# One weight pool throughout, a down product that begins in freed tiles of h, x loaded once, gate and up interleaved k by k, and lo parts on GpSimd

## The chip, the cores and the metric

The kernel runs on one core of a Trainium2 chip. The metric is device microseconds of one execution. Before the change the median of three runs is 3011.32 us (3008.94 to 3018.25). The execution that was profiled took 3016.26 us, and its trace spans 3014.5 us.

## The reference

One decoder layer for 1024 tokens of width 1024, everything in float32. What matters here are the two SwiGLU layers (d_ff 2816, 22 blocks of 128 columns) at its two ends; between them lie three mixers that the change touches only through the weight pool.

```python
def _swiglu(h, w_gate, w_up, w_down):
    return (jax.nn.silu(h @ w_gate) * (h @ w_up)) @ w_down
...
    x = x + 0.5 * _swiglu(_rmsnorm(x, ffn1_norm[l]), ffn1_w_gate[l], ffn1_w_up[l], ffn1_w_down[l])
    h = _rmsnorm(x, mix_norm[l])
    p_rwkv, q_nsa, kv_nsa, g_nsa, q_mem, g_branch = _split(h @ w_in[l], IN_SPLITS)
    ...
    merged = (gb[:, :, 0] * (y_rwkv @ w_br_rwkv[l]) + gb[:, :, 1] * (y_nsa @ w_br_nsa[l]) + gb[:, :, 2] * (y_mem @ w_br_mem[l]))
    x = x + merged @ w_out[l]
    x = x + 0.5 * _swiglu(_rmsnorm(x, ffn2_norm[l]), ffn2_w_gate[l], ffn2_w_up[l], ffn2_w_down[l])
return _rmsnorm(x, final_norm)
```

## The kernel before

**Precision.** Every operand of a matmul is a pair: `split` (L74) writes the rounded value `hi` on ScalarE (L77) and the rest `lo = src - hi` on VectorE (L80). A product is three matmuls (`mm3`, L95: hi by hi L97, hi by lo L98, lo by hi L99). All tokens of a tile lie along the free axis, 512 ("a half") at a time, so nearly every instruction is on 128x512.

**Weights.** `wload` fetches a raw 128x512 piece over SP's queue (L84, tile `wraw`) and splits it into `whi`, `wlo`. The pool is opened anew by `open_w` (L60) for each of three stretches: 8 raw buffers and 4 pairs in the first SwiGLU, 2 and 3 in the mixers, 8 and 4 in the second SwiGLU. What is opened anew lies in memory that tiles of the stretch before used until then.

**A SwiGLU layer.** `Gates.plain` (L290) does the blocks f = 0 and 1 for one half of the tokens, gate and then up, eight k each. `Gates.sums` (L304) then makes, from h of both halves, four sums and differences of 128x512 tiles for each of four k (three on GpSimd, L311, L312, L314; one on VectorE, L313) and splits them into the tiles t1 to t4. `Gates.run` (L347) takes the other 20 blocks as seven products P1 to P7 in place of eight; P1, P2 and P3 read h, P5, P6, P7 and P4 read t1, t2, t3, t4. The block's weights need such sums too (`blocks`, L324, GpSimd, tiles `wS`). Results go as `sg` to DRAM (`ad<-sg`, L288). PSUM tiles are called `pgu`.

**Down.** `tail` (L185) reads `ad` back and splits it into tiles `a`, in four chunks (L21: 5 blocks in tiles of their own, 8 in the tiles of h, 5, and 4 in the tiles of h again). Per chunk and per d (eight blocks of 128 output columns) it multiplies with the down weights into PSUM tiles `pd` (four banks) and adds them to x in SBUF (L221). All eight tiles of x are loaded (L1496, L1702; 512 KB each) ahead of the first chunk.

**Start.** x's first half is loaded into ring tiles `rg`, normed without its rstd (`hu`), and used by `plain(0)`. x's second half is loaded when ring tiles come free, its squares are added up on GpSimd (L110), `rstd` (L113) has TensorE sum them over partitions (`nps`), and `plain(1)` follows. For the sums the first half is loaded a second time.

**Before the second SwiGLU.** The last rows of the merge (`h<-gbt`, L1589) are followed by the product with w_out (`wo`, weights from `in_wo`), into the ring again.

**Order.** A scheduler orders the instructions of each engine's queue from the program's tiles and pools; each engine then works its queue strictly in order. SP's queue issues nearly all DMAs.

Of the kernel before, what the change touches and what calls it, by code (L numbers as in the profile page):

```python
# [8 lines left out]
FT = mybir.dt.float32  # L9
# [8 lines left out]
D = 1024  # L18
KT = 8
HALF = 512  # L20
CHUNKS = (("p", 5), ("h", 8), ("p", 5), ("t", 4))  # L21
RING = 10
AHEAD = 3

# [4 lines left out]
class Builder:  # L29
    def __init__(self, ctx, tc, A):  # L30
        self.ctx, self.tc, self.nc, self.A = ctx, tc, tc.nc, A
        self.cst = ctx.enter_context(tc.tile_pool(name="cst", bufs=1))
        self.hp = ctx.enter_context(tc.tile_pool(name="hp", bufs=1))
        self.bg = []
        self.consts()
# [21 lines left out]
        self.eps = self.cst.tile([128, 1], FT, name="eps")  # L57
        nc.vector.memset(self.eps, 1e-6)

    def open_w(self, st, raw=2, parts=3):  # L60

        self.wp = st.enter_context(self.tc.tile_pool(name="wp", bufs=1, reuse_waits="tile"))
        self.wbufs = raw, parts

    def load_consts(self):
        nc, A = self.nc, self.A
# [13 lines left out]
        (nc.vector if eng_lo == "dve" else nc.gpsimd).tensor_sub(lo, src, hi.bitcast(FT))  # L80

    def wraw(self, src, n):
        raw = self.wp.tile([128, n], FT, name="wraw", tag="wraw", bufs=self.wbufs[0])
        self.nc.sync.dma_start(raw, src)  # L84
        return raw

    def wparts(self, raw, eng_lo="dve", eng_hi="act"):
        hi, lo = [self.wp.tile([128, raw.shape[-1]], FR, name=t, tag=t, bufs=self.wbufs[1]) for t in ("whi", "wlo")]
        self.split(hi, lo, raw, eng_hi, eng_lo)
        return hi, lo  # L90

# [93 lines left out]
    def tail(self, x, wd, ad, xload, after, aside=None, st=None):  # L185

        nc = self.nc
        halves = [slice(0, HALF), slice(HALF, S)]
        ap = st.enter_context(self.tc.tile_pool(name="ffa", bufs=1, reuse_waits="tile"))
        ps = st.enter_context(self.tc.tile_pool(name="ffd", bufs=1, space=PSUM, reuse_waits="tile"))  # L190

        def parts(kind, j):

            if kind == "p":
                return [[ap.tile([128, HALF], FR, name=f"a{p}{j}{half}") for p in range(2)] for half in range(2)]
            a, b = (1, j) if kind == "t" else divmod(j, 4)
            return [[self.hp.tile([128, HALF], FR, name=f"a{p}{j}{half}", tag=f"h{p}{a}{2 * b + half}")
                     for p in range(2)] for half in range(2)]

        def loads(kind, f0, n):  # L200
            got = []
            for j in range(n):
                t = parts(kind, j)
                for half in range(2):
                    raw = self.wraw(ad[f0 + j][half], HALF)
                    self.split(*t[half], raw)
                got.append(t)
                yield got

        def down(d, f0, a, hs):  # L210
            w = []
            for q0 in range(0, len(a), 4):
                q1 = min(q0 + 4, len(a))
                w.append(self.wload(wd[d, :, (f0 + q0) * 128:(f0 + q1) * 128], (q1 - q0) * 128))
            for half in hs:
                p = ps.tile([128, HALF], FT, name="pd", tag="dn", bufs=4)
                for j, t in enumerate(a):
                    wc = slice((j % 4) * 128, (j % 4) * 128 + 128)
                    self.mm3(p, [b[:, wc] for b in w[j // 4]], t[half], j == 0, j == len(a) - 1)
                c = halves[half]  # L220
                nc.vector.scalar_tensor_tensor(x[d][:, c], p, 0.25, x[d][:, c], op0=OP.mult, op1=OP.add)  # L221

        f0 = 0
        gens, at = [], []
        for kind, n in CHUNKS:
            gens.append(loads(kind, f0, n))
            at.append(f0)
            f0 += n
        a = [None] * len(CHUNKS)
        for a[0] in gens[0]:  # L230
            pass
        for d in range(KT):
            xload(d)
        for ci, (kind, n) in enumerate(CHUNKS):
            if ci < len(CHUNKS) - 1:
                for d in range(KT):
                    down(d, at[ci], a[ci], (0, 1))
                    a[ci + 1] = next(gens[ci + 1], a[ci + 1])
                    if aside and ci:
                        next(aside, None)  # L240
                if aside and ci:
                    for _ in aside:
                        pass
            else:
                for half in range(2):
                    for d in range(KT):
                        down(d, at[ci], a[ci], (half,))
                        self.tick()
                        after(half, d)


class Gates:
# [37 lines left out]
    def plain(self, half, h, r=lambda: None, loads=None, step=None):  # L290

        B = self.B
        for f in range(2):
            for gu in range(2):
                w = [loads.pop(0) if loads else B.wload(self.wgu[f, gu, q], 512) for q in range(2)]
                ps = self.bank()
                for k in range(KT):
                    wc = slice((k % 4) * 128, (k % 4) * 128 + 128)
                    B.mm3(ps, [a[:, wc] for a in w[k // 4]], h[k], k == 0, k == KT - 1)
                if step:  # L300
                    step()
                self.finish(f, half, gu, ps, r())

    def sums(self, h, k, raw):  # L304


        B, nc = self.B, self.nc
        a11, a12, a21, a22 = raw
        add = nc.gpsimd
        out = []  # L310
        add.tensor_sub(a11, a12, a11)  # L311
        add.tensor_sub(a12, a22, a12)  # L312
        nc.vector.tensor_sub(a22, a22, a11)  # L313
        add.tensor_sub(a21, a21, a22)  # L314
        for n, a in ((1, a11), (2, a22), (3, a12)):
            t = [self.tp.tile([128, HALF], FR, name=f"t{p}{n}{k}") for p in range(2)]
            B.split(*t, a)
            out.append(t)
        t = [B.hp.tile([128, HALF], FR, name=f"t{p}4{k}", tag=f"h{p}1{k}") for p in range(2)]
        B.split(*t, a21)  # L320
        out.append(t)
        return out

    def blocks(self, m):  # L324
# [1067 lines left out]
def body(ctx, tc, A, VO):  # L1392
# [44 lines left out]

    with ExitStack() as fs:
        with ExitStack() as st:
            B.open_w(fs, 8, 4)  # L1440
            ring = ring_of(st)
            F = Gates(B, st, ring, A["wgu1"], ad)
            g1 = VO["ffn1_norm"]
            hu, h = ([], []), ([], [])

            def loadx(half, k):
                t = ring()
                nc.sync.dma_start(t, A["xT"][k][:, halves[half]])
                return t

            xt, early, acc = [], [], None
            for k in range(KT):
                xt.append(loadx(0, k))
                if k in LOADS:
                    early.append(B.wload(A["wgu1"][0, LOADS[k][0], LOADS[k][1]], 512))
            for k in range(KT):
                t = F.temp()
                nc.vector.tensor_scalar(t, xt[k], B.vec[:, g1 + k:g1 + k + 1], None, op0=OP.mult)
                B.split(*B.htile(hu, 0, k), t)
                acc = B.add_square(np_, acc, xt[k], nc.gpsimd)  # L1460
            r = {}

            def more():
                if not r:
                    r[0] = B.rstd(np_, nps, acc)

            F.plain(0, hu[0], lambda: r[0], early, more)
            B.load_consts()
            xt, acc = [], None
            for k in range(KT):  # L1470
                xt.append(loadx(1, k))
                acc = B.add_square(np_, acc, xt[k], nc.gpsimd)
            r[1] = B.rstd(np_, nps, acc)
            for k in range(KT):
                B.normed(xt[k], xt[k], r[1], g1 + k)
                B.split(*B.htile(h, 1, k), xt[k])
            F.plain(1, h[1])
            sums, late = [], []
            for k in range(4):
                two = []  # L1480
                for j in (k, k + 4):
                    t = loadx(0, j)
                    B.normed(t, t, r[0], g1 + j)
                    hj = [B.hp.tile([128, HALF], FR, name=f"h{p}0{j}", tag=f"h{p}0{j}") for p in range(2)]
                    B.split(*hj, t)
                    two.append((hj, t))
                h[0].insert(k, two[0][0])
                h[0].append(two[1][0])
                sums.append(F.sums(h, k, (two[0][1], xt[k], two[1][1], xt[k + 4])))
            F.run(h, sums)  # L1490
        mt = met.enter_context(tc.tile_pool(name="met", bufs=1, side="right", reuse_waits="tile"))
        xp = xs.enter_context(tc.tile_pool(name="xp", bufs=1, side="right", reuse_waits="tile"))
# [6 lines left out]
                   M.tokens(mt, np_, nps, VO["mem_norm"]), st)  # L1499

    with ExitStack() as mid:
        B.open_w(mid)
        B.mmp = mid.enter_context(tc.tile_pool(name="mmp", bufs=1, space=PSUM, reuse_waits="tile"))
        gp = mid.enter_context(tc.tile_pool(name="gp", bufs=1, reuse_waits="tile"))
        sp = Spill(B, drp, A)
# [119 lines left out]

    with ExitStack() as fs:
        np_, nps = B.norm_pool(fs)
        B.open_w(fs, 8, 4)
        with ExitStack() as st:
            ring = ring_of(st)  # L1630
            xt, r, h = {}, {}, ([], [])
# [153 lines left out]
```

## Time and profile before

| | us |
|---|---|
| median of three runs | 3011.32 (3008.94 to 3018.25) |
| the profiled execution | 3016.26 |
| its span in the trace | 3014.5 |
| TensorE busy | 2842.3 (94 %) |
| VectorE, ScalarE, GpSimd busy | 1772.1, 1289.0, 640.7 (59, 43, 21 %) |

TensorE is busy 94 % of the span, in stretches that are wholly full and a few that are not. In the page's 40 slices the thin ones are the first two, the seventh, the 29th, the 37th and the last: the start, the two changes from gates to down, w_out and the sums, and the end. In a full stretch a matmul of 128x512 takes 0.2267 us (24 of them, one product of 4 blocks for two halves, 5.44 us).

### The profile page before, as it was taken

The page shows a single profiled execution, that of the slowest core. Times are in us where ns is not written, and L with a number is a line of the kernel's source. Part 1 is how long each engine was busy: PE and PEld are TensorE (multiplying, and loading weights), DVE is VectorE, ACT ScalarE, POOL GpSimd, SP SyncE. Part 2 cuts the span into 40 slices and gives each one's busy share as a digit, 9 for nine tenths or more (in the row PEclk, how much of TensorE's full clock was granted, in tenths as well). Part 3 has the DMA queues.
Part 4 walks back from the last instruction along what each step waited for, and adds up shares of the span by engine and source line. Part 5 has one row for each costly group of instructions (what it writes and reads, how often), then busy time and mean ns, then how long its engine had stood idle before and what let it go on. Part 6 is the DMA issues. An engine that isn't in the chain of part 4 may idle for free. (4 is left out here: it accounts for less than half of the span.)

```text
span 3014.5 us, 39899 instructions
## 1 busy us (share of the span) xinstructions
PE 2842.3 (94%) x13728; PEld 2252.2 (75%) x13728; DVE 1772.1 (59%) x3825; ACT 1289.0 (43%) x2752; POOL 640.7 (21%) x724
## 2 busy tenths in 40 slices
PE   6899997999999999999999989999899899997997
PEld 4588885888887677776767667777787688885886
DVE  6755554445566566666555357888756655554336
ACT  5433333223454345544443356666544433333213
POOL 3422220002212011111110133333223422220002
PEclk8799998999999999999999999999999899998998
DMA  4222225423313122222221552221564222225222
GB/s 165 70 84 84 83 82 179 132 77 114 118 53 92 58 76 61 74 72 64 62 64 62 157 163 74 81 72 58 184 189 156 79 84 84 84 84 192 92 74 86
DMA packets 201895, 295.46 MB, mean 98 GB/s; under 512 B 46003, under 2 KB 73531, under 8 KB 201692
## 3 DMA queue, kind: packets, MB, share of 16 engines
q1 hardware_dynamic: 185232, 264.30, 28.1%
q10 hardware_dynamic: 16460, 28.61, 3.2%
q8 instruction: 108, 1.77, 0.2%
q14 instruction: 95, 0.78, 0.1%
HBM read 224.56 MB, written 68.27 MB: 97 GB/s over the span
## 5 line engine op out<-in xcount | busy, mean ns | idle before, releaser
L77 ACT ACTIVATE whi<-wraw 128x512 fp32r<-128x512 f32 (+1 forms) x564 | 343.8, 612 | 828.1 <-PE pgu L98 266.8
L80 DVE TENSOR_TENSOR wlo<-wraw,whi 128x512 fp32r<-128x512 f32 (+1 forms) x556 | 396.0, 714 | 411.9 <-ACT whi L77 355.2
L97 PE MATMUL mm<-h,whi 128*128 128x512 f32 x800 | 330.3, 413 | 0.2 <-ACT gbt L1520 0.2
L99 PE MATMUL mm<-h,wlo 128*128 128x512 f32 x800 | 320.5, 401 | 7.2 <-DVE wlo L80 7.2
L98 PE MATMUL mm<-h,whi 128*128 128x512 f32 x800 | 318.3, 398 | 0.0
L97 PE MATMUL pd<-a,whi 128*128 128x512 f32 x704 | 276.1, 392 | 38.5 <-ACT whi L77 38.5
L99 PE MATMUL pd<-a,wlo 128*128 128x512 f32 x704 | 275.4, 391 | 0.6 <-DVE wlo L80 0.6
L98 PE MATMUL pd<-a,whi 128*128 128x512 f32 x704 | 275.5, 391 | 0.0
L97 PE MATMUL pgu<-t,whi 128*128 128x512 f32 x640 | 253.7, 396 | 7.7 <-ACT t L77 4.5
L99 PE MATMUL pgu<-t,wlo 128*128 128x512 f32 x640 | 252.4, 394 | 5.6 <-DVE wlo L80 5.6
L97 PE MATMUL pgu<-h,whi 128*128 128x512 f32 x608 | 241.7, 398 | 15.0 <-ACT h L77 13.8
L98 PE MATMUL pgu<-t,whi 128*128 128x512 f32 x640 | 252.8, 395 | 3.0 <-DVE t L80 3.0
L98 PE MATMUL pgu<-h,whi 128*128 128x512 f32 x608 | 242.4, 399 | 11.9 <-DVE h L80 11.9
L99 PE MATMUL pgu<-h,wlo 128*128 128x512 f32 x608 | 239.8, 395 | 1.2 <-DVE wlo L80 1.2
L110 POOL TENSOR_TENSOR acc<-acc,sq 128x512 f32<-128x512 f32 x53 | 77.7, 1465 | 508.4 <-ACT sq L109 503.2
L97 PEld LDWEIGHTS pd<-a,whi 128*128 128x128 f32 x704 | 133.2, 189 | 66.8 <-ACT whi L77 39.4
L99 PEld LDWEIGHTS mm<-h,wlo 128*128 128x128 f32 x800 | 151.5, 189 | 39.9 <-DVE wlo L80 8.8
L97 PEld LDWEIGHTS mm<-h,whi 128*128 128x128 f32 x800 | 151.8, 190 | 36.1 <-issue 5.3
L98 PEld LDWEIGHTS mm<-h,whi 128*128 128x128 f32 x800 | 151.9, 190 | 28.5 <-issue 3.0
L221 DVE SCALAR_TENSOR_TENSOR x<-pd,x 128x512 f32<-128x512 f32 x128 | 87.9, 687 | 129.3 <-PE pd L99 129.2
L99 PEld LDWEIGHTS pd<-a,wlo 128*128 128x128 f32 x704 | 133.0, 189 | 29.3 <-DVE wlo L80 1.5
L98 PEld LDWEIGHTS pd<-a,whi 128*128 128x128 f32 x704 | 133.3, 189 | 27.8
(393 smaller groups left out, 6103.3 us busy)
## 6 DMA issues: line engine op xcount, KB each, us to landing
wraw<-in_wgu SPq DMA_DIRECT2D x192, 256.0 KB, 2.7
wraw<-in_wd SPq DMA_DIRECT2D x96, 256.0 KB, 2.8
ad<-sg SPq DMA_DIRECT2D x88, 256.0 KB, 2.7
wraw<-ad SPq DMA_DIRECT2D x88, 256.0 KB, 2.8
wraw<-in_win SPq DMA_DIRECT2D x52, 256.0 KB, 2.6
wraw<-in_wgb SPq DMA_DIRECT2D x48, 256.0 KB, 2.8
gd<-gbt SPq DMA_DIRECT2D x48, 256.0 KB, 2.0
gbt<-gd ACTq DMA_DIRECT2D x40, 256.0 KB, 2.7
```

The source lines that it names most:

```text
L77: nc.scalar.activation(hi, src, AF.Copy)
L80: (nc.vector if eng_lo == "dve" else nc.gpsimd).tensor_sub(lo, src, hi.bitcast(FT))
L97: mm(ps, w[0], x[0], start=start, stop=False, **kw)
L98: mm(ps, w[0], x[1], start=False, stop=False, **kw)
L99: mm(ps, w[1], x[0], start=False, stop=stop, **kw)
L110: eng.tensor_add(acc, acc, sq)
L221: nc.vector.scalar_tensor_tensor(x[d][:, c], p, 0.25, x[d][:, c], op0=OP.mult, op1=OP.add)
```

## The change

One pool `wp` (2 raw, 3 pairs) is opened once for the whole program; the SwiGLU layers add a second pool `wx` (6 raw, 1 pair), and `wtile` deals tiles from both in turn. The chunks of `tail` become 4 blocks in the tiles of h (of the first half), 5 in tiles of their own, 8 in h, 5; x's first tile is loaded before the first chunk and each other one behind a d of it. In the first SwiGLU x's first half goes into the tiles that t3 takes later (`x0k`), is normed in place and not loaded again; the second half's loads stand right behind the first's. `plain` interleaves gate and up k by k and calls `step` once per f. In `sums` the lo parts of t3 and t4, and in the first SwiGLU those of every second tile of the second half's h, go to GpSimd.

```diff
-CHUNKS = (("p", 5), ("h", 8), ("p", 5), ("t", 4))
+CHUNKS = (("a", 4), ("p", 5), ("h", 8), ("p", 5))
...
+        self.wp = ctx.enter_context(tc.tile_pool(name="wp", bufs=1))
...
-        self.wp = st.enter_context(self.tc.tile_pool(name="wp", bufs=1, reuse_waits="tile"))
-        self.wbufs = raw, parts
+        self.wx, self.wn = st.enter_context(self.tc.tile_pool(name="wx", bufs=1, reuse_waits="tile")), [0, 0]
...
+    def wtile(self, tags, n, dt):
+
+        base, more, i = (2, 6, 0) if len(tags) == 1 else (3, 1, 1)
+        pool, bufs = self.wp, base
+        if self.wx:
+            if self.wn[i] % (base + more) >= base:
+                pool, bufs = self.wx, more
+            self.wn[i] += 1
+        return [pool.tile([128, n], dt, name=t, tag=t, bufs=bufs) for t in tags]
...
-        for d in range(KT):
-            xload(d)
+        xload(0)
         for ci, (kind, n) in enumerate(CHUNKS):
             if ci < len(CHUNKS) - 1:
                 for d in range(KT):
                     down(d, at[ci], a[ci], (0, 1))
+                    if ci == 0 and d < KT - 1:
+                        xload(d + 1)
...
         for f in range(2):
+            w = [[loads.pop(0) if loads else B.wload(self.wgu[f, gu, q], 512) for q in range(2)] for gu in range(2)]
+            ps = [self.bank() for _ in range(2)]
+            for k in range(KT):
+                wc = slice((k % 4) * 128, (k % 4) * 128 + 128)
+                for gu in range(2):
+                    B.mm3(ps[gu], [a[:, wc] for a in w[gu][k // 4]], h[k], k == 0, k == KT - 1)
...
-        for n, a in ((1, a11), (2, a22), (3, a12)):
-            t = [self.tp.tile([128, HALF], FR, name=f"t{p}{n}{k}") for p in range(2)]
-            B.split(*t, a)
...
+        for n, a, eng in ((1, a11, "dve"), (2, a22, "dve"), (4, a21, "pool"), (3, a12, "pool")):
+            pool, tag = (B.hp, lambda p: f"h{p}1{k}") if n == 4 else (self.tp, lambda p: f"t{p}{n}{k}")
+            t = out[n - 1] = [pool.tile([128, HALF], FR, name=f"t{p}{n}{k}", tag=tag(p)) for p in range(2)]
+            B.split(*t, a, eng_lo=eng)
...
-                t = ring()
+                t = ring() if half else F.tp.tile([128, HALF], FT, name=f"x0{k}", tag=f"t{k // 4}3{k % 4}")
                 nc.sync.dma_start(t, A["xT"][k][:, halves[half]])
...
+            for k in range(KT):
+                xt[1].append(loadx(1, k))
...
+                                B.split(*B.htile(h, 1, k), xt[1][k], eng_lo="pool" if k % 2 else "dve")
...
-                    t = loadx(0, j)
+                    t = xt[0][j]
                     B.normed(t, t, r[0], g1 + j)
```

SP's queue where the first SwiGLU goes from gates to down, before: `ad211`, `ad210` and `ad201` are the last results of the gates, x0 to x7 the tiles of x, `in_wd1` the down weights, `ad40` to `ad51` blocks read back.

```order
L288 DMA ad211_191<-sg_3722 128x512
L288 DMA ad210_190<-sg_3766 128x512
L288 DMA ad201_189<-sg_3808 128x512
L84 DMA wraw_3968<-ad40_156 128x512
L84 DMA wraw_3972<-ad41_157 128x512
L1496 DMA x0_3902<-in_xT 128x1024
...
L1496 DMA x7_3909<-in_xT 128x1024
L84 DMA wraw_3984<-in_wd1 128x512
L84 DMA wraw_3990<-in_wd1 128x128
L84 DMA wraw_4034<-ad50_158 128x512
```

The same place after the change:

```order
L100 DMA wraw_3952<-in_wd1 128x512
...
L100 DMA wraw_3999<-in_wd1 128x512
L305 DMA ad200_191<-sg_3623 128x512
...
L100 DMA wraw_4046<-in_wd1 128x512
...
L305 DMA ad211_194<-sg_3709 128x512
L305 DMA ad210_193<-sg_3753 128x512
L100 DMA wraw_4136<-ad71_166 128x512
L305 DMA ad201_192<-sg_3795 128x512
L100 DMA wraw_4093<-in_wd1 128x512
L100 DMA wraw_4140<-in_wd1 128x512
L1509 DMA x0_3889<-in_xT 128x1024
L1509 DMA x1_3890<-in_xT 128x1024
```

The weights of d = 0, 1 and 2 (`wraw_3952`, `wraw_3999`, `wraw_4046`) and the blocks of the first chunk have moved ahead of the last results of the gates; x0 to x5 follow those results as before, but with the weights of d = 3 and 4 ahead of them. The second SwiGLU has the same pattern.

GpSimd's queue at the start, from the weights' sums of the first products on, before:

```order
L332 TENSOR_TENSOR wS_908<-wraw_896,wraw_898 128x512
L333 TENSOR_TENSOR wS_909<-wS_908,wraw_892 128x512
L336 TENSOR_TENSOR wraw_896<-wraw_892,wraw_896 128x512
L332 TENSOR_TENSOR wS_1044<-wraw_962,wraw_964 128x512
L336 TENSOR_TENSOR wraw_962<-wraw_958,wraw_962 128x512
L339 TENSOR_TENSOR wraw_894<-wraw_894,wS_909 128x512
L333 TENSOR_TENSOR wS_1045<-wS_1044,wraw_958 128x512
L311 TENSOR_TENSOR rg_756<-rg_502,rg_756 128x512
L312 TENSOR_TENSOR rg_502<-rg_521,rg_502 128x512
L314 TENSOR_TENSOR rg_763<-rg_763,rg_521 128x512
```

The same stretch after the change, a part of it (L96 is `split`'s lo part, L329 to L332 the sums):

```order
L347 TENSOR_TENSOR wS_895<-wraw_883,wraw_885 128x512
L348 TENSOR_TENSOR wS_896<-wS_895,wraw_879 128x512
L351 TENSOR_TENSOR wraw_883<-wraw_879,wraw_883 128x512
L329 TENSOR_TENSOR x00_235<-rg_275,x00_235 128x512
L329 TENSOR_TENSOR x01_243<-rg_277,x01_243 128x512
L96 TENSOR_TENSOR h111_472<-rg_277,h011_471 128x512
L96 TENSOR_TENSOR h113_482<-rg_281,h013_481 128x512
L330 TENSOR_TENSOR rg_275<-rg_283,rg_275 128x512
...
L96 TENSOR_TENSOR t140_782<-x04_255,t040_781 128x512
L96 TENSOR_TENSOR t130_786<-rg_275,t030_785 128x512
...
L96 TENSOR_TENSOR t143_872<-x07_267,t043_871 128x512
L96 TENSOR_TENSOR t133_876<-rg_281,t033_875 128x512
```

From `wS_895` to `t133` GpSimd's queue holds 31 instructions of 128x512, where before it held 19 from `wS_908` to the last sum; 12 of them are lo parts (4 of h, 8 of t3 and t4) that stood in VectorE's queue. The sums now stand ahead of the lo parts of h that `plain(1)` needs.

SP's queue ahead of w_out, before (`yd131<-yo` are the last blocks of a mixer's result, `in_wo` the weights of w_out):

```order
L84 DMA wraw_21030<-in_wbr 128x512
L1619 DMA yd131_91<-yo_20836 128x128
L1619 DMA yd131_91<-yo_20991 128x128
L84 DMA wraw_21111<-in_wo 128x512
L84 DMA wraw_21117<-in_wo 128x512
```

The same place after the change:

```order
L100 DMA wraw_21062<-in_wbr 128x512
L1631 DMA yd131_94<-yo_20868 128x128
L100 DMA wraw_21142<-in_wo 128x512
L100 DMA wraw_21148<-in_wo 128x512
L100 DMA wraw_21308<-in_wo 128x512
L1631 DMA yd131_94<-yo_21023 128x128
```

Three loads of w_out's weights have moved ahead of the last block of the mixer.

## Rows read from the trace of the kernel before

**Rows 1.** The page's line on busy time.

```profile
PE 2842.3 (94%) x13728; PEld 2252.2 (75%) x13728; DVE 1772.1 (59%) x3825; ACT 1289.0 (43%) x2752; POOL 640.7 (21%) x724
```

**Rows 2.** What TensorE waited for over the whole span, by line and releaser: us in total, times, longest us.

```profile
PE pd L97 <- ACT whi L77: 38.5, 2, 19.5
PE nps L122 <- ACT sqh L77: 15.9, 3, 10.2
PE pgu L97 <- ACT h L77: 13.8, 5, 5.9
PE pgu L98 <- DVE h L80: 11.9, 10, 2.9
PE wo L97 <- ACT whi L77: 8.2, 1, 8.2
```

**Rows 3.** Stretches of 20 us: the length, then busy us (instructions) of PE, PEld, DVE, ACT and POOL, the granted clock of TensorE as a share, the DMA share and GB/s.

```profile
80.00:100.00 20.00, 10.38 (x21) 4.83 (x19) 17.59 (x21) 8.11 (x13) 10.06 (x8) 0.59 0.28 91
100.00:120.00 20.00, 14.64 (x35) 9.02 (x35) 16.98 (x21) 9.84 (x18) 9.73 (x6) 0.56 0.09 25
...
500.00:520.00 20.00, 10.91 (x39) 8.79 (x40) 8.14 (x15) 7.22 (x14) 0.00 (x0) 0.66 0.88 320
520.00:540.00 20.00, 20.00 (x90) 16.57 (x89) 12.40 (x22) 7.66 (x14) 0.00 (x0) 1.00 0.57 179
...
2340.00:2360.00 20.00, 12.21 (x26) 7.34 (x27) 20.00 (x21) 9.98 (x17) 11.37 (x8) 0.59 0.20 64
...
2740.00:2760.00 20.00, 8.65 (x28) 6.94 (x29) 6.11 (x11) 5.63 (x11) 0.00 (x0) 0.60 0.94 339
```

**Rows 4.** TensorE in order of time where gates give way to down, in the first SwiGLU and in the second: start us, duration, line, tiles, count, and in brackets the idle time before with what ended it.

```profile
489.67 0.39 PE L99 MATMUL pgu<-h,wlo 128*128 128x512 f32 x1
...
509.09 0.80 PE L97 MATMUL pd<-a,whi 128*128 128x512 f32 x1 [19.03 <-ACT whi L77]
...
513.10 0.58 PE L97 MATMUL pd<-a,whi 128*128 128x512 f32 x1
513.52 0.39 PE L98 MATMUL pd<-a,whi 128*128 128x512 f32 x1
...
2731.47 0.39 PE L99 MATMUL pgu<-h,wlo 128*128 128x512 f32 x1
...
2751.35 0.80 PE L97 MATMUL pd<-a,whi 128*128 128x512 f32 x1 [19.49 <-ACT whi L77]
```

**Rows 5.** SP's DMA issues there, in order of time.

```profile
493.16 5.09 SPq L1496 DMA_DIRECT2D x<-in_xT  x8
498.45 1.67 SPq L84 DMA_DIRECT2D wraw<-in_wd  x2
...
2735.14 5.00 SPq L1702 DMA_DIRECT2D x<-x2d  x8
2741.10 1.64 SPq L84 DMA_DIRECT2D wraw<-in_wd  x2
```

**Rows 6.** ScalarE's first split of a down weight in the first SwiGLU, with the wait before it.

```profile
508.41 0.83 ACT L77 ACTIVATE whi<-wraw 128x512 fp32r<-128x512 f32 x2 [11.54 <-DMA wraw<-in_wd]
```

**Rows 7.** DMA from 485 to 512 us: the total, and two kinds of issue with KB each and the median us from issue to landing.

```profile
DMA packets 3190, 7.49 MB, mean 278 GB/s; under 512 B 344, under 2 KB 634, under 8 KB 3188
...
x<-in_xT SPq DMA_DIRECT2D x8, 512.0 KB, 8.5
```

**Rows 8.** w_out's beginning: SP, TensorE and ScalarE, each in order of time.

```profile
2147.04 10.88 SPq L1619 DMA_DIRECT2D yd<-yo  x2
2160.16 9.01 SPq L84 DMA_DIRECT2D wraw<-in_wo  x6
...
2161.18 0.39 PE L99 MATMUL mm<-y,wlo 128*128 128x512 f32 x1
2169.75 0.80 PE L97 MATMUL wo<-h,whi 128*128 128x512 f32 x1 [8.19 <-ACT whi L77]
...
2165.43 0.63 ACT L77 ACTIVATE h<-gbt 128x512 fp32r<-128x512 f32 x1 [3.50 <-DMA yr<-yd]
...
2169.07 0.63 ACT L77 ACTIVATE whi<-wraw 128x512 fp32r<-128x512 f32 x1 [0.79 <-DVE y L80]
```

**Rows 9.** GpSimd and VectorE in order of time during the second SwiGLU's sums; then one GpSimd sum after them, when VectorE had few instructions, and two VectorE subtractions at the start while GpSimd was idle.

```profile
2342.45 1.32 POOL L314 TENSOR_TENSOR rg<-rg 128x512 f32<-128x512 f32 x1 [2.17 <-DVE rg L313]
2343.73 1.71 POOL L311 TENSOR_TENSOR rg<-rg 128x512 f32<-128x512 f32 x1
2345.52 1.59 POOL L312 TENSOR_TENSOR rg<-rg 128x512 f32<-128x512 f32 x1
...
2341.95 5.71 DVE L80 TENSOR_TENSOR t<-rg,t 128x512 fp32r<-128x512 f32 x4
...
2361.17 1.27 POOL L339 TENSOR_TENSOR wraw<-wraw,wS 128x512 f32<-128x512 f32 x1 [4.90 <-DVE wlo L80]
...
64.33 1.29 DVE L80 TENSOR_TENSOR h<-rg,h 128x512 fp32r<-128x512 f32 x2
```

**Rows 10.** The start, in order of time: TensorE's first matmul of rstd and of plain(1), GpSimd's additions of squares, VectorE's first normed tiles of the second half, and its last four splits of the sums.

```profile
49.24 0.80 PE L122 MATMUL nps<-sqh,ones 128*128 128x512 f32 x1 [10.20 <-ACT sqh L77]
...
56.28 1.22 PE L97 MATMUL pgu<-h,whi 128*128 128x512 f32 x2 [5.13 <-ACT h L77]
...
40.19 8.34 POOL L110 TENSOR_TENSOR acc<-acc,sq 128x512 f32<-128x512 f32 x6 [0.61 <-ACT sq L109]
...
54.81 2.08 DVE L147 SCALAR_TENSOR_TENSOR rg<-rg,vec,rst 128x512 f32<-128x512 f32 x3
...
113.28 3.57 DVE L80 TENSOR_TENSOR t<-rg,t 128x512 fp32r<-128x512 f32 x4
```

**Rows 11.** One group of the page's kind, with shapes kept apart: the lo parts that GpSimd already makes in the mixers. Busy us, mean ns of one, idle us before.

```profile
L80 POOL TENSOR_TENSOR wlo<-wraw,whi 128x512 fp32r<-128x512 f32 x8 | 10.9, 1364 | 10.8 <-ACT whi L77 8.2 <-DMA wraw<-in_mwk 2.6
```

More of the change, by code (lines that the diff above doesn't have):

```diff
@@ L32, in __init__ @@
         self.cst = ctx.enter_context(tc.tile_pool(name="cst", bufs=1))
+        self.wp = ctx.enter_context(tc.tile_pool(name="wp", bufs=1))
+        self.wx, self.wn = None, [0, 0]
         self.hp = ctx.enter_context(tc.tile_pool(name="hp", bufs=1))
@@ L58, in consts, with more_w, end @@
         nc.vector.memset(self.eps, 1e-6)
-    def open_w(self, st, raw=2, parts=3):
-        self.wp = st.enter_context(self.tc.tile_pool(name="wp", bufs=1, reuse_waits="tile"))
-        self.wbufs = raw, parts
+    def more_w(self, st):
+        self.wx, self.wn = st.enter_context(self.tc.tile_pool(name="wx", bufs=1, reuse_waits="tile")), [0, 0]
+        def end():
+            self.wx = None
+        st.callback(end)
+    def wtile(self, tags, n, dt):
[6 more added lines that the diff above has]
+        return [pool.tile([128, n], dt, name=t, tag=t, bufs=bufs) for t in tags]
     def load_consts(self):
@@ L82, in wraw @@
     def wraw(self, src, n):
-        raw = self.wp.tile([128, n], FT, name="wraw", tag="wraw", bufs=self.wbufs[0])
+        raw, = self.wtile(("wraw",), n, FT)
         self.nc.sync.dma_start(raw, src)
@@ L87, in wparts @@
     def wparts(self, raw, eng_lo="dve", eng_hi="act"):
-        hi, lo = [self.wp.tile([128, raw.shape[-1]], FR, name=t, tag=t, bufs=self.wbufs[1]) for t in ("whi", "wlo")]
+        hi, lo = self.wtile(("whi", "wlo"), raw.shape[-1], FR)
         self.split(hi, lo, raw, eng_hi, eng_lo)
@@ L293, in plain @@
         for f in range(2):
-            for gu in range(2):
[L295 to L302, printed above, removed]
+            w = [[loads.pop(0) if loads else B.wload(self.wgu[f, gu, q], 512) for q in range(2)] for gu in range(2)]
[4 more added lines that the diff above has]
+                    B.mm3(ps[gu], [a[:, wc] for a in w[gu][k // 4]], h[k], k == 0, k == KT - 1)
+            if step:
+                step()
+            for gu in range(2):
+                self.finish(f, half, gu, ps[gu], r())
     def sums(self, h, k, raw):
@@ L309, in sums @@
         add = nc.gpsimd
-        out = []
+        out = [None] * 4
         add.tensor_sub(a11, a12, a11)
@@ L314, in sums @@
         add.tensor_sub(a21, a21, a22)
-        for n, a in ((1, a11), (2, a22), (3, a12)):
-            t = [self.tp.tile([128, HALF], FR, name=f"t{p}{n}{k}") for p in range(2)]
-            B.split(*t, a)
[L318 to L321, printed above, removed]
+        for n, a, eng in ((1, a11, "dve"), (2, a22, "dve"), (4, a21, "pool"), (3, a12, "pool")):
+            pool, tag = (B.hp, lambda p: f"h{p}1{k}") if n == 4 else (self.tp, lambda p: f"t{p}{n}{k}")
+            t = out[n - 1] = [pool.tile([128, HALF], FR, name=f"t{p}{n}{k}", tag=tag(p)) for p in range(2)]
+            B.split(*t, a, eng_lo=eng)
         return out
@@ L1439, in body @@
         with ExitStack() as st:
-            B.open_w(fs, 8, 4)
+            B.more_w(fs)
             ring = ring_of(st)
@@ L1446, in loadx @@
             def loadx(half, k):
-                t = ring()
+                t = ring() if half else F.tp.tile([128, HALF], FT, name=f"x0{k}", tag=f"t{k // 4}3{k % 4}")
                 nc.sync.dma_start(t, A["xT"][k][:, halves[half]])
                 return t
-            xt, early, acc = [], [], None
+            xt, early, acc, r = [[], []], [], [None, None], {}
             for k in range(KT):
-                xt.append(loadx(0, k))
+                xt[0].append(loadx(0, k))
                 if k in LOADS:
@@ L1456, in body @@
             for k in range(KT):
+                xt[1].append(loadx(1, k))
+            for k in range(KT):
                 t = F.temp()
-                nc.vector.tensor_scalar(t, xt[k], B.vec[:, g1 + k:g1 + k + 1], None, op0=OP.mult)
+                nc.vector.tensor_scalar(t, xt[0][k], B.vec[:, g1 + k:g1 + k + 1], None, op0=OP.mult)
                 B.split(*B.htile(hu, 0, k), t)
[L1460 to L1465, printed above, removed]
@@ L1467, in body @@
-            F.plain(0, hu[0], lambda: r[0], early, more)
-            B.load_consts()
[L1469 to L1476, printed above, removed]
+                acc[0] = B.add_square(np_, acc[0], xt[0][k], nc.gpsimd)
@@ new lines, in step @@
+            def step():
+                for half in range(2):
+                    if half not in r:
+                        if half:
+                            for k in range(KT):
+                                acc[1] = B.add_square(np_, acc[1], xt[1][k], nc.gpsimd)
+                        r[half] = B.rstd(np_, nps, acc[half])
+                        if half:
+                            for k in range(KT):
+                                B.normed(xt[1][k], xt[1][k], r[1], g1 + k)
+                                B.split(*B.htile(h, 1, k), xt[1][k], eng_lo="pool" if k % 2 else "dve")
@@ L1477, in body @@
+            F.plain(0, hu[0], lambda: r[0], early, step)
+            B.load_consts()
             F.plain(1, h[1])
-            sums, late = [], []
+            sums, top = [], []
             for k in range(4):
-                two = []
-                for j in (k, k + 4):
-                    t = loadx(0, j)
+                for j, to in ((k, h[0]), (k + 4, top)):
+                    t = xt[0][j]
                     B.normed(t, t, r[0], g1 + j)
[L1484 to L1489, printed above, removed]
+                    to.append([B.hp.tile([128, HALF], FR, name=f"h{p}0{j}", tag=f"h{p}0{j}") for p in range(2)])
+                    B.split(*to[-1], t)
+                sums.append(F.sums(h, k, (xt[0][k], xt[1][k], xt[0][k + 4], xt[1][k + 4])))
@@ L1490, in body @@
+            h[0].extend(top)
             F.run(h, sums)
@@ L1501, in body @@
     with ExitStack() as mid:
-        B.open_w(mid)
         B.mmp = mid.enter_context(tc.tile_pool(name="mmp", bufs=1, space=PSUM, reuse_waits="tile"))
@@ L1627, in body @@
         np_, nps = B.norm_pool(fs)
-        B.open_w(fs, 8, 4)
+        B.more_w(fs)
         with ExitStack() as st:
```

2 lines of the change are left out of this document (1 added, 1 removed).

## The prediction

> **What bounds the kernel now.** I read the page's busy line first: TensorE is busy 2842 of 3014.5 us [rows 1], so at most some 170 us can come from idle time, and the change removes no matmul. Then TensorE's waits [rows 2], where one line towers over the rest: the down product waited twice for a split weight, 38.5 us in all. The other entries that the change touches are the start (`nps`, h) and w_out, 8.2 us in one wait. The stretches of 20 us [rows 3] show where that time lies: a full stretch has 90 matmuls at clock 1.00 (0.2222 us each; 0.2267 between starts in the rows), the poor ones have 21 to 39, at granted clocks of 0.56 to 0.66. A hole so costs twice: the hole, and the matmuls behind it that run at the lower level.
>
> *The change from gates to down.* The last matmul of the gates starts at 489.67, the first of down at 509.09 [rows 4]. SP's queue [rows 5] tells why: eight loads of x (4 MB) stand ahead of the first down weight. They are issued at 493.16, when the gates' memory comes free, the weight at 498.45, and it is split at 508.41 [rows 6], since all share the 16 DMA engines: 7.49 MB at 278 GB/s [rows 7]. The second SwiGLU repeats it.
>
> *The sums.* In these stretches VectorE is full and TensorE starves [rows 3]. I looked at GpSimd and VectorE together [rows 9]: a GpSimd sum takes 1.27 us when VectorE leaves it alone and up to 1.71 beside VectorE; four VectorE subtractions take 5.71 us beside three GpSimd sums, two take 1.29 when GpSimd is idle. They take turns: 5.71 − 3 × 1.27 leaves 1.90 for four, 0.48 each. The same two numbers fill the stretches: 8 × 1.27 + 21 × 0.48 = 20.2 of the 20 us from 2340, and (8 + 6) × 1.27 + (21 + 21) × 0.48 = 37.9 of the 40 us from 80. So here the sum of both engines' work is the bound, not the longer of the two.
>
> **The change part by part** (gains in us).
>
> *Gates to down, first SwiGLU.* The new order has the first chunk's blocks and the weights of d = 0, 1 and 2 ahead of the last gates, in tiles of h that P1 and P2 have left (72 matmuls before the end, 16 us). The first chunk needs nothing of the last product, so down can follow directly. What goes: 19.0 us of hole, and ten matmuls that took 4.43 us (509.09 to 513.52) instead of 2.27: 2.2 us [rows 4]. Together 21.2. What is late next is x. It still waits for the gates' memory, so x0 is issued some 3.5 us after the last gate matmul, as in [rows 4, 5]. Its sum is queued on VectorE, and behind it lie later splits; four PSUM banks let TensorE run two d, 2 × 5.44 = 10.9 us, without it. Alone x0 needs a few us, in the crowd of [rows 7] the median was 8.5: it lands 7 to 12 us after the last gate matmul, and costs 0 to 1 us. Each further d gives 5.44 us, and 512 KB take 1.9 us at 278 GB/s. The down weight of d = 5, behind x0 to x5, has over 20 us. Bounds: 15 (6 us lost to late x, below) to 21.2. I take 20.5, near the end where the queue is served in order.
>
> *The same in the second SwiGLU.* 19.5 + 2.2 = 21.7 [rows 4], bounds 15.5 to 21.7; I take 21.
>
> *w_out.* Two weight pieces now come ahead of the last mixer block, because their buffers need no fresh memory. In the hole of 8.2 us, the first product of w_out (24 matmuls, 5.4 us) can run; its last three matmuls need the h that is split at 2165.43 [rows 8]. The next product needs y tiles that are read back as late as before, or later: `yd131` is now behind three more issues, at 9.01 / 6 = 1.5 us each [rows 8], 4.5 us. Bounds 1 (5.5 − 4.5) to 8.2; I take 5.5.
>
> *The start.* x's second half lands sooner, so the squares need not run from 40.19 to 48.5 [rows 10], but plain(1) then meets the next link: weights' splits, tanh and rstd in the queues of ScalarE and VectorE. By the order I put rstd's end at 50.8, against 54.8 before, so 4 us earlier. From there GpSimd has 31 instructions to the last t3 (19 before), VectorE 41 with two SBUF inputs. In turns that is 31 × 1.27 + 41 × 0.48 = 59.1 us, to 109.9; before, the last split ended at 116.9 [rows 10]. But now nearly all of P6, P5 and P7, some 34 matmuls, are still to come behind it, at 0.22 to 0.43 us some 9 us: 119, where the old order reaches the same place at about 120. Bounds: −5 (lo parts on GpSimd at the 1.364 us of [rows 11] and h of plain(1) late behind the sums in its queue) to +15 (half of the overlap in the first rival and an earlier rstd). I take +2. Gate and up k by k brings nothing of its own: before, up ran while rstd was awaited.
>
> The Trainium skill, SBUF — State Buffer, section "Who interferes with whom", says that a VectorE instruction with two SBUF inputs contends with a GpSimd instruction that reads SBUF, and that the loser blocks wholly. By that rule a lo part moved to GpSimd hands the pair 1.27 us of exclusive use for 0.48 saved, and the start gains about nothing; the trace agrees (1.43 us for each of four subtractions beside three sums, 0.60 alone).
>
> *The second SwiGLU's sums.* GpSimd 22 and VectorE 15 instead of 13 and 26: 22 × 1.27 + 15 × 0.48 = 35.1 us against 29.0; they end 6 us later, but t1 and t2 are ready sooner, so TensorE has less left to do. By the order both are at the same matmul near 2369. 0, bounds −5 to +5.
>
> *The rest.* The new chunks need eight small weight loads more per tail, beside full TensorE stretches with DMA at 0.57 [rows 3]; the mixers' TensorE order is unchanged. 0, bounds −2 to +2.
>
> Sum: 2 + 20.5 + 5.5 + 0 + 21 = 49. The profiled execution took 3016.26, so 2967 in its terms; the median of the runs is 4.9 lower: **2962**.
>
> **The rivals.**
>
> *A: GpSimd and VectorE overlap after all.* Then the start's sums last as long as GpSimd alone: 31 × 1.27 = 39.4, to 90; plus the 9 us of matmuls 99 instead of 120, a gain of 20, and the second sums gain 3. For it: single GpSimd sums of 1.27 us stand in the crowded stretch too (1.32 at 2342.45). Against it: both stretches add up [rows 3, 9]. 20 + 20.5 + 5.5 + 3 + 21 = 70: 2941.
>
> *B: the holes move rather than close.* x0 to x5 and their neighbours share the engines, so that x0 lands with the crowd: some 3.7 MB at 278 GB/s, 13.4 us after the issue, 16.9 us after the last gate matmul, where TensorE can go 10.9. A stall of 6 us in each tail: gain 49 − 12 = 37, 2974. For it: the median landing of 8.5 us where one of eight loads should need far less [rows 7]. Against it: the weights split at 508.41 came about when 4 MB had passed, so the queue is served about in order.
>
> *C: GpSimd's queue becomes the bound, and the kernel slower.* The sums stand ahead of the lo parts of h in GpSimd's queue, and each waits for tiles of VectorE, which waits in turn. Its pace in the old sums was 40 us for 14 instructions [rows 3], 2.86 each, where my sum has 59.1 / 31 = 1.91 and 35.1 / 22 = 1.60. The loss is 53 p − 94 at pace p; it eats the other gains (47) from p = 2.67 on, and at 2.86 the kernel is 10 us slower: 3021. Against it: VectorE was the one with more work then, and that work is what leaves its queue.
>
> *D: it doesn't do what it says.* If the first chunk's tiles or the new weight tiles still waited for the gates' end, half of each hole would stay: 49 − 20 = 29, 2982. Against it: the order of SP shows the loads ahead of the last results.
>
> **How the numbers follow.** Forecast 0.58 (2950 to 2972 by its own), A 0.12, B 0.18, D 0.08, C 0.04. From 2940 (A; all upper bounds together give 71 us) to 2980 lies what is between A and beyond B; some of D and all of C are left out. 0.3 % (9 us) is about what a measurement of this kernel tells from no change: faster than that 0.95, within it 0.03, slower 0.02 (half of C, which starts at even).
>
> **What would show it.** Right: no wait of `pd` above 3 us, TensorE near 20 us of 20 across both changes to down with clock about 1; `wo` waits under 3 us at first; the 120-us state reached at 115 to 122; GpSimd's t3 and t4 splits at 1.3 to 1.7 us, VectorE's instructions beside them above 1 us. Wrong: `pd` waits at the third d for an addition to x (B), a wait for the first `whi` (D), a last t3 split before 100 (A) or after 125 us (C), or mixers that last some us longer or shorter, for which I have no term.

## The result, and the profile after

The changed kernel took 2972.64 us, the median of four runs (2970.09 to 2979.31), against 3014.78 for the kernel before in the same comparison: a ratio of 0.9865, 95 % interval 0.9839 to 0.9891. The forecast was 2962, with 2940 to 2980 around it. The profiled execution took 2979.31 us (span 2977.5), the slowest of the four. The stages below add up to 37.0 us, which is what lies between these two executions; the medians lie 42.1 apart.

Cut at events that both traces have, the two profiled executions compare like this (ends and starts of groups of matmuls; us):

| stage | before | after | gained | forecast |
|---|---|---|---|---|
| start to the last gate matmul, first SwiGLU | 490.1 | 490.1 | 0.0 | 2 |
| down, first SwiGLU | 261.7 | 241.3 | 20.4 | 20.5 |
| mixers, to the last matmul of attention (`O`) | 1404.7 | 1407.4 | −2.7 | 0 |
| from there to the end of w_out | 127.9 | 122.9 | 5.0 | 5.5 |
| gates, second SwiGLU | 447.5 | 457.5 | −10.0 | 0 |
| down, second SwiGLU | 262.7 | 241.5 | 21.2 | 21 |
| behind the last down matmul | 19.9 | 16.8 | 3.1 | 0 |

TensorE's waits after the change, us in total, times, longest; they answer to [rows 2]:

```profile
PE pgu L113 <- ACT h L93: 14.5, 3, 8.1
PE pgu L115 <- DVE wlo L96: 9.0, 8, 3.1
PE pgu L114 <- DVE t L96: 8.8, 6, 2.3
PE pgu L113 <- ACT rg L385: 8.6, 3, 6.6
PE nps L138 <- ACT sqh L93: 8.4, 2, 5.5
...
PE wo L113 <- ACT whi L93: 4.4, 1, 4.4
...
PE pd L115 <- DVE wlo L96: 1.7, 2, 1.4
```

The line of 38.5 us is gone; of `pd` 1.7 us are left. Everything at the top now is the start and the sums.

The change from gates to down in order of time (TensorE, SP, VectorE), which answers to [rows 4, 5]:

```profile
489.70 0.39 PE L115 MATMUL pgu<-h,wlo 128*128 128x512 f32 x1
489.93 0.39 PE L113 MATMUL pd<-a,whi 128*128 128x512 f32 x1
...
492.18 1.04 SPq L100 DMA_DIRECT2D wraw<-in_wd  x2
493.31 3.67 SPq L1509 DMA_DIRECT2D x<-in_xT  x6
...
499.53 2.65 DVE L237 SCALAR_TENSOR_TENSOR x<-pd,x 128x512 f32<-128x512 f32 x4 [1.95 <-DMA x<-in_xT]
```

Down starts 0.23 us behind the last gate matmul, at full clock. x0 is requested at 493.31 and is there at 499.5; VectorE's first addition to x waits for it 1.95 us, and TensorE does not, since two d last to 500.8. The addition that frees the first bank ends at 500.2, so the margin is 0.6 us.

The crowded stretches, columns as in [rows 3]:

```profile
80.00:100.00 20.00, 15.08 (x53) 11.48 (x54) 20.00 (x16) 9.49 (x16) 16.94 (x12) 0.78 0.15 43
100.00:120.00 20.00, 13.45 (x47) 10.54 (x46) 14.78 (x15) 7.50 (x14) 14.80 (x10) 0.74 0.19 63
...
500.00:520.00 20.00, 20.00 (x90) 16.57 (x89) 9.86 (x16) 4.43 (x7) 0.00 (x0) 1.00 0.81 303
...
2320.00:2340.00 20.00, 10.64 (x27) 6.22 (x27) 12.02 (x9) 7.58 (x13) 18.65 (x13) 0.79 0.31 96
2340.00:2360.00 20.00, 14.70 (x48) 10.78 (x49) 11.13 (x11) 8.04 (x14) 11.07 (x8) 0.70 0.05 14
```

Where [rows 3] had 39 matmuls from 500 to 520, there are 90. From 80 to 100 VectorE is shown busy all the time, but with 16 instructions, where the stretch of before had 21 in 17.6 us: an instruction's length there holds its wait for GpSimd. The sums of the second SwiGLU now fill 2312 to 2349, 36.5 us; before, 2329 to 2358, 28.9 (in the page's slices of the kernel before that is the 31st and 32nd, not the 29th). There the two engines have changed places: GpSimd is busy for 33.5 of the 36.5 us, and VectorE is idle for 12.6, most of it (9.8) in waits for GpSimd's sums like this one:

```profile
2341.99 1.74 DVE L331 TENSOR_TENSOR rg<-rg 128x512 f32<-128x512 f32 x1 [4.95 <-POOL rg L330]
```

### The profile page after: what moved, and what is told of

Read it like the earlier page. It is cut to its first block, busy times and chain, and to the rows that moved or that the text cites. A ratio compares the mean times of both kernels' runs of the same rounds, so it can differ in the third digit from the quotient of the medians.

```text
span 2977.5 us, 39927 instructions
## 1 busy us (share of the span) xinstructions
PE 2832.6 (95%) x13728; PEld 2246.5 (75%) x13728; DVE 1790.7 (60%) x3821; ACT 1291.1 (43%) x2768; POOL 675.0 (23%) x744
## 5 line engine op out<-in xcount | busy, mean ns | idle before, releaser
L93 ACT ACTIVATE whi<-wraw 128x512 fp32r<-128x512 f32 x580 | 348.1, 603 | 764.0 <-PE pgu L114 282.0
L96 DVE TENSOR_TENSOR wlo<-wraw,whi 128x512 fp32r<-128x512 f32 (+1 forms) x572 | 415.5, 729 | 378.1 <-ACT whi L93 356.2
L113 PEld LDWEIGHTS mm<-h,whi 128*128 128x128 f32 x800 | 152.4, 190 | 36.5 <-issue 5.3
L114 PEld LDWEIGHTS mm<-h,whi 128*128 128x128 f32 x800 | 152.6, 191 | 28.9 <-issue 3.0
L113 PEld LDWEIGHTS pgu<-h,whi 128*128 128x128 f32 x608 | 116.5, 192 | 49.5 <-ACT h L93 15.9
L113 PEld LDWEIGHTS pgu<-t,whi 128*128 128x128 f32 x640 | 121.6, 190 | 42.3 <-ACT rg L385 10.1
```

The costliest lines, as they stand in the source:

```text
L93: nc.scalar.activation(hi, src, AF.Copy)
L113: mm(ps, w[0], x[0], start=start, stop=False, **kw)
L114: mm(ps, w[0], x[1], start=False, stop=False, **kw)
```

## The experiments

Two theories stood against each other on the sums. **T**: GpSimd and VectorE take turns, and the sum of both is the length. **R** or **A**: they overlap, and the loss comes from elsewhere. On the holes, T says that the first chunk's tiles and the order of SP's queue close them. I read the stages rather than the totals: in the nine profiled executions whose order on TensorE is the same through the mixers, these took 1398 to 1410 us, so a single total is uncertain by more than some of the terms. A stage is uncertain too: with one and the same order on TensorE the first SwiGLU's gates ended at 487.8 to 490.1 in five executions, and the second's took 457.0 to 459.3 in four, so 2 us of a stage say nothing.

**Lo parts back on VectorE.**

```diff
-        for n, a, eng in ((1, a11, "dve"), (2, a22, "dve"), (4, a21, "pool"), (3, a12, "pool")):
+        for n, a, eng in ((1, a11, "dve"), (2, a22, "dve"), (4, a21, "dve"), (3, a12, "dve")):
...
-                                B.split(*B.htile(h, 1, k), xt[1][k], eng_lo="pool" if k % 2 else "dve")
+                                B.split(*B.htile(h, 1, k), xt[1][k])
```

> The changed kernel (2972.6 us), but all lo parts of t3, t4 and of h back on VectorE; the sums stay on GpSimd. Theory T (GpSimd and VectorE take turns, 1.27 us and 0.48 us each, and the sum of both is the length of the sums' stretches): second SwiGLU's gates 457 to about 448 us, start (first SwiGLU's gates end at 490.1) 9 us earlier since 31 x 1.27 + 41 x 0.48 = 59 becomes 19 x 1.27 + 53 x 0.48 = 50; total about 2954 (2950 to 2962). Rival R (the 10 us lost in the second SwiGLU's gates come from gate and up k by k, or from the loads' order): 2968 to 2978, gates of the second SwiGLU still 455 or more.

Measured 2968.09 (ratio to before 0.9843, 0.9824 to 0.9863). The first SwiGLU's gates end at 482.3, 7.8 us earlier (T: 9). The second SwiGLU's gates take 455.2, only 2.3 us less (T: 9). T holds at the start; in the second SwiGLU the number is R's, and so is the total. The trace tells both apart: from the first sum to the last split it is 29.4 us instead of 36.5, as T has it, but the first sum begins 52.8 us behind w_out, where it was 44.7 before the change. Something else holds the beginning up.

**Gate, then up.** Only `plain` goes back.

> The changed kernel with gate and up in plain one after the other again (step still once per gate or up). Theory T: nothing hangs on it, 2970 to 2976; second SwiGLU's gates still about 457 us. Rival R: gates of the second SwiGLU back to 448, total about 2963.

Measured 2969.45 (0.985, 0.9823 to 0.9877). The second SwiGLU's gates take 452.8, and the first sum begins 44.9 us behind w_out instead of 50.6. So R is half right: k by k makes the sums begin later. How it does so is shown in part. In the changed kernel GpSimd's first sum of weights begins 35.3 us behind w_out, here 31.6, and the tokens' first sum follows such a sum without a pause. But with the sums on VectorE, away from GpSimd's queue, they begin just as late (51.9 us with k by k, 44.9 without, in two runs below), so that queue is not the whole cause. That k by k holds every weight pair of an f to its end, and the next block's pairs come later, is a guess from the code.

**Both together.**

> The kernel of the run that the throttled clock spoiled, once more: lo parts on VectorE, gate then up, sums on GpSimd. If the lo parts on GpSimd and gate and up k by k make up the 10 us by which the second SwiGLU's gates grew (447.5 to 457.5), these come to 447 to 449 us; if they stay at 451 or more, something else in the change costs there.

Measured 2957.87 (0.9824, 0.9795 to 0.9852), second gates 445.5: the two edits are the whole loss, and 2.0 us more, which is within the scatter. The first sum begins at 44.9 and the last split ends at 73.6 us behind w_out, to two tenths as in the kernel before (44.7 and 73.6). A first run of this kernel took 4769 us (last section); nothing on the sums is read from it.

**All sums on VectorE too** (`add = nc.vector` on top of the first experiment).

> As the run before it, and the twelve sums of each SwiGLU on VectorE too; GpSimd keeps only the weights' sums. Theory T: a GpSimd instruction costs the pair 1.27, a VectorE one 0.48 to 0.60, so another 8 to 10 us at the start and 5 to 8 in the second SwiGLU: about 2942 (2935 to 2955). Rival V (VectorE becomes the bound once it has all): not faster than the run before, 2955 to 2970.

Measured 2955.14 (0.9805, 0.9784 to 0.9825); the first SwiGLU's gates end at 479.9, the second's take 447.3. The total lies on the border of both forecasts, so the stages decide. The second SwiGLU's gates gain 7.9 us (T: 5 to 8), the start only 2.4 (T: 8 to 10): its last split comes 5.5 us earlier, and TensorE has more matmuls left behind it. V falls: VectorE has all of it, and no stage of the sums is longer than with both engines. But T's prices are wrong, as the start shows. VectorE's queue in the second SwiGLU, and GpSimd's in the same stretch:

```profile
2303.93 0.69 DVE L332 TENSOR_TENSOR rg<-rg 128x512 f32<-128x512 f32 x1
2304.53 0.69 DVE L96 TENSOR_TENSOR t<-rg,t 128x512 fp32r<-128x512 f32 x1
2305.13 1.76 DVE L329 TENSOR_TENSOR rg<-rg 128x512 f32<-128x512 f32 x1
2306.82 1.78 DVE L96 TENSOR_TENSOR t<-rg,t 128x512 fp32r<-128x512 f32 x1
2308.51 0.68 DVE L330 TENSOR_TENSOR rg<-rg 128x512 f32<-128x512 f32 x1
...
2304.91 1.43 POOL L347 TENSOR_TENSOR wS<-wraw 128x512 f32<-128x512 f32 x1 [11.42 <-DMA wraw<-in_wgu]
2306.42 1.62 POOL L351 TENSOR_TENSOR wraw<-wraw 128x512 f32<-128x512 f32 x1
```

0.60 us from start to start alone; beside each of the two weight sums of GpSimd one instruction takes 1.70 from start to start. So in these rows a VectorE instruction costs 0.60 us, and a GpSimd instruction beside it 1.10 more, not 0.48 and 1.27. Four subtractions in 5.71 us beside three sums [rows 9] are 4 × 0.60 + 3 × 1.10 = 5.7 as well. The two pairs of prices part where GpSimd has little: here the start has 6 GpSimd and 68 VectorE instructions from the first normed tile to the last split, 40.3 us by the old prices, 47.4 by the new, and the trace has 47.7. In the second SwiGLU (2 and 36) it is 19.8, 23.8 and 24.0. For the changed kernel's start (31 and 47) they hardly differ: 61.9, 62.3 and 59.8. Where VectorE is the bound, an instruction that goes back to it so gains 0.5 us, not 0.8.

**GpSimd work that nobody reads.** One execution. On top of the last kernel, in the second SwiGLU's `sums`; it adds eight instructions and leaves the computation as it is:

```diff
+        if dum is not None:
+            for b in (a11, a12):
+                nc.gpsimd.tensor_sub(dum, b, a22)
```

> As the run with all lo parts and sums on VectorE, and in the second SwiGLU's sums eight more GpSimd subtractions of 128x512 into a tile that nobody reads (no part of the computation). Theory T (the two engines take turns): VectorE's chain grows by up to 8 x 1.27 = 10 us, gates of the second SwiGLU from 447 to 452 to 457 us, VectorE's subtractions beside them 1.3 to 1.8 us. Rival A (they overlap): GpSimd has the time, gates stay at 446 to 449 us.

The second SwiGLU's gates take 456.2 instead of 447.3: 8.9 us for eight instructions, 1.1 each. Nobody reads their results; they cost by being there. VectorE's starts in the two traces are equal to a hundredth for the twelve instructions ahead of the first pair. With it (GpSimd, VectorE):

```profile
2297.25 3.34 POOL L339 TENSOR_TENSOR dum<-rg 128x512 f32<-128x512 f32 x2 [3.76 <-DVE rg L331]
...
2297.69 1.78 DVE L332 TENSOR_TENSOR rg<-rg 128x512 f32<-128x512 f32 x1
2299.39 2.95 DVE L96 TENSOR_TENSOR t<-rg,t 128x512 fp32r<-128x512 f32 x3
```

Without it (VectorE):

```profile
2297.69 0.68 DVE L332 TENSOR_TENSOR rg<-rg 128x512 f32<-128x512 f32 x1
2298.30 1.89 DVE L96 TENSOR_TENSOR t<-rg,t 128x512 fp32r<-128x512 f32 x3
```

A is refuted here: the four VectorE instructions end at 2302.3 instead of 2300.2, one wait of a microsecond for each of the two. Three loads of the next tiles do wait for the eight, which hold the ring tiles that they read (5.4 us of SP's time), but VectorE is never idle for more than 0.3 us in either run while the sums last, so that delay costs nothing here. The Trainium skill, SBUF — State Buffer, section "Who interferes with whom", has this rule (two SBUF inputs on VectorE against a GpSimd instruction that reads SBUF; the loser blocks), and this run agrees, with 8.9 us.

**Which part closes the holes.** Four kernels in a square, old or new chunks by old or new place of x's loads; the one pool of weights is in all. The three others are one execution each.

> The changed kernel with both the old chunks (5, 8, 5 in own tiles or h, 4 last) and all loads of x ahead of the first down weight; the one weight pool stays. Theory T (the first chunk's tiles and the place of x close the holes): waits of pd near 19 us back, each tail 261 to 263 us instead of 241, and the end behind the last down matmul back from 16.8 to about 19.9 us (last chunk 4 blocks instead of 5): total about 3016. Rival P (the pool does it): tails near 241.

> New chunks, but all eight loads of x requested ahead of the first chunk. Theory T: the down weights of the first d still stand ahead of x in SP's queue, because their tiles are free earlier, so the tails stay at 241 to 246 us. Rival X (x's place in the program is what counts): tails 252 to 262.

> Old chunks, x interleaved with the first chunk. Theory T: the first chunk's tiles wait for the gates' memory, and x0 alone instead of eight tiles stands ahead of the first weight: a hole of 6 to 12 us at each change, tails 248 to 255 us. Rival X: tails near 241.

| down of the two SwiGLUs, us | x ahead of all | x behind each d |
|---|---|---|
| old chunks | 263.0, 261.4 (3016.03 in all) | 252.3, 251.8 (2998.11) |
| new chunks | 241.3, 241.5 (2980.65) | 241.3, 241.5 (the change) |

TensorE's wait for the first down weight, both with old chunks, first x ahead, then x behind each d:

```profile
PE pd L113 <- ACT whi L93: 38.7, 2, 20.0
```

```profile
PE pd L113 <- ACT whi L93: 18.8, 2, 9.5
```

With the new chunks x's place is worth nothing: the down weights have left the queue before x comes up. With the old ones it is worth half of each hole, and the other half stays, because the weights are requested behind the last gate result (at 491.33 in the first SwiGLU, the last gate matmul starting at 487.36). Old chunks also bring back 19.0 and 19.5 us behind the last down matmul (16.8 with new ones). Old and new chunks differ in the first chunk's size as well as in its place (5 blocks in tiles of their own, 4 in freed tiles of h); that the place does it is argued from the order of the requests, not tested apart.

**The pool.** `open_w` back in three places, all else as changed.

> The changed kernel with the weight pool opened anew for each stretch, as before (8 and 4, 2 and 3, 8 and 4). Theory T: the two changes from gates to down stay closed (the chunk in freed tiles of h does it, and the weights' pool is the same within a SwiGLU), w_out's first wait goes from 4.4 back to about 8 us: 2974 to 2981. Rival P (the pool that stays open is what closes the holes): waits of pd near 19 us are back, about 3013.

Measured 2977.65 (0.9885, 0.9862 to 0.9909). Both tails stay short (241.3 and 241.9), and w_out's wait is back:

```profile
2156.95 0.79 PE L102 MATMUL wo<-h,whi 128*128 128x512 f32 x1 [8.40 <-ACT whi L82]
```

From the last `O` to the end of w_out it takes 127.7 us, against 121 to 123 in every kernel with one pool; in the stages of the two SwiGLUs there is no more than 1.2 us between the two. The mixers took 1413.3 us, 5.9 more, but in an execution that was 10 us longer than the other three of its kernel, and with an order on TensorE of their own; whether the pool costs anything there stays open. At w_out it is worth 4 to 7 us, and the medians of the two kernels lie 5 apart. P falls.

**All on VectorE, gate then up.**

> All lo parts and sums on VectorE, and gate then up in plain. If the costs of the two edits in the second SwiGLU's gates add up (457.5 in the changed kernel, 447.3 with all on VectorE, 452.8 with gate then up), they come to about 443 us, and the first SwiGLU's gates end near 478: total 2944 to 2952. If they overlap, 447 us and 2952 to 2958.

Measured 2952.71 (0.9804, 0.9787 to 0.9821). The second gates take 441.6, so there the costs add up; the first SwiGLU's gates end at 484.1, not near 478 as expected, 4 us later than with k by k, and the total is outside of the 2944 to 2952 of that case. There k by k pays: plain(0) ends near 38 instead of near 50 us, and plain(1) begins at 54.4 instead of 57.0.

**Each where it is shorter.** k by k in the first SwiGLU, gate then up in the second, sums and lo parts on VectorE.

> All lo parts and sums on VectorE; gate and up k by k in the first SwiGLU, one after the other in the second. Each part from the run where it was shorter: first SwiGLU's gates end at 480 (as with all on VectorE), second SwiGLU's gates 441.6 (as with gate then up): 4 to 6 us under the run with all on VectorE, 2946 to 2952.

Measured 2947.31, median of five (2945.31 to 2955.50), ratio to before 0.9782 (0.9764 to 0.9801): the lowest median, 25 us under the changed kernel; its interval overlaps that of the run before it. The first SwiGLU's gates end at 479.8, the second's take 439.5 us. A stretch of its start, columns as in [rows 3]:

```profile
80.00:100.00 20.00, 7.13 (x25) 5.18 (x24) 20.00 (x30) 8.77 (x15) 5.28 (x3) 0.67 0.08 27
100.00:120.00 20.00, 20.00 (x89) 16.50 (x88) 10.51 (x16) 8.69 (x15) 9.59 (x6) 0.99 0.18 53
```

VectorE does 30 instructions in the 20 us in which it did 16 beside GpSimd, and TensorE, which has only 25 matmuls there, is full from 100 on.

## Why the prediction was right, and where it was not

The forecast's range held, and the two largest terms held by their mechanism. The total owes something to luck: it is 10.6 us above the 2962, 10.0 lost in a stage put at 0, and 3.1 gained at the end by a step that the prediction did not have. By the total alone rival B (2974) would be nearer; the stages decide against it.

**The holes** were right to a few tenths: 20.4 and 21.2 against 20.5 and 21, late x included (it lands 9.8 us behind the start of the last gate matmul, stated as 7 to 12). B and D are out: the longest wait of `pd` is 1.4 us, for a `wlo`. The clock came back with the hole, as the step had it.

**w_out** was right, 5.0 against 5.5: its first product begins 4.8 us behind the last `O` instead of 13.2, and the second waits 4.4 us. That wait was to stay under 3, so this sign failed. The cause, memory that needs no release, had been inferred from the order, and the run with reopened pools shows it.

**The start** gained 0.0 against 2, which is within the scatter of this stage. The turns gave 59.1 us; the trace has 59.8, from the first normed tile at 53.8 to the last split at 113.6. That it came out so well is in part luck: of its two prices one is too high and the other too low, and in this mix they balance. What slipped was rstd: 53.3 instead of 50.8. The additions of squares on GpSimd met VectorE as well (six in 10.05 us, against 8.34 in [rows 10]), and from the second half's first `nps` matmul to its first normed tile it now takes 9.1 us instead of 5.6; which of the two counts was not tested.

**The second SwiGLU's sums** are where the forecast failed: 0 with bounds of 5, and 10.0 us lost. Its length came near (35.1 stated, 36.5 measured), but not as it was added up: GpSimd's queue is the bound there, with VectorE idle for 12.6 us. Two steps failed. "Gate and up k by k brings nothing of its own" was worked out for the start alone; in the second SwiGLU it makes the sums begin 5.9 us later. And "they end 6 us later, but t1 and t2 are ready sooner, so TensorE has less left to do" was taken as an even trade: behind the last split, up to the 400th matmul, TensorE needed 39.1 us before and 35.2 after, 3.9 us less, against 7.6 us of added length. 5.9 + 7.6 − 3.9 = 9.6 of the 10.0 us.

**The end** gained 3.1 us that no step had. The last chunk has five blocks instead of four, so a d takes 3.4 instead of 2.7 us, and VectorE and GpSimd keep up. The last addition of squares, before and after:

```profile
2998.36 0.69 DVE L110 TENSOR_TENSOR acc<-acc,sq 128x512 f32<-128x512 f32 x1 [1.56 <-POOL acc L110]
```

```profile
2962.27 0.69 DVE L126 TENSOR_TENSOR acc<-acc,sq 128x512 f32<-128x512 f32 x1 [0.82 <-ACT sq L125]
```

It ends 4.5 us behind the last down matmul before, and 2.2 after; the other 0.9 us were not looked for. That the chunks do this is shown by the two runs with old ones; that it is the blocks per d, and not another of their properties, is argued from these rows.

**C** is out in its price (GpSimd's pace was 59.8 / 31 = 1.9 us at the start and 36.5 / 22 = 1.7 in the second SwiGLU, not 2.86: in the 40 us that gave this price GpSimd was busy for 19.8) but right in its direction. In the second SwiGLU GpSimd's queue did become the bound, and what was moved to GpSimd costs, as k by k does. A is refuted by the eight idle instructions. **The mixers'** 2.7 us lie within what they differ by between executions; TensorE's order there, put as unchanged, differs in 96 of the first 117 matmuls, out of 7374. The upper bounds add up to 73 us, not 71, with the 2 of the rest; no chance hangs on it.

## What to carry to other kernels

- Before moving an elementwise instruction from VectorE to GpSimd to relieve it, look whether VectorE's instructions beside GpSimd's are longer than alone (here 1.75 against 0.68 us). If they are, a GpSimd instruction costs VectorE this extra length (here 1.1 us) on top of its own work, so count both engines' instructions, and try the move the other way.
- When two phases share memory, let the second begin in tiles that the first has finished with early; then, as here, the weights' requests overtake by themselves, and the order of the large loads no longer matters.
- The same edit can pay in one stage and cost in another: price it in each place where the function is called.

## What the runs showed that was not expected

Eight GpSimd instructions whose result nobody reads cost 8.9 us of the kernel. The mixers take 1398 to 1410 us in nine executions with the same order on TensorE there; what varies in them was not tried. And one execution took 4769 us, of a kernel whose next two took 2955.89 and 2959.86. For its first 1225 us the clock is shown as granted in full (1.00), yet a matmul of 128x512 took 0.46 us there from start to start instead of 0.227; after that the granted clock is 0.555 and a matmul took 0.40. So the granted clock (0.67 in the mean) does not tell the whole of it. Other kernels ran at a mean clock of 0.967 to 0.983 on the same chip in the same session; what slowed this one stays open.
